# A two-layer hybrid encoder trunk in 32-bit floats: keys and gate inputs turned through memory, one offset product in the last norm, readers pinned and GpSimd in program order

## The chip, the cores and the metric

The kernel runs on one core of one Trainium2 chip. The metric is the device time of one execution in microseconds (us), as the median over several runs. TensorE (PE in the profile), VectorE (DVE), ScalarE (ACT) and GpSimd (POOL) are the core's compute engines; SyncE (SP) issues transfers, and ScalarE and GpSimd can do so as well.

## The reference, cut to what matters

Two layers of one block. One input projection feeds three groups of heads, each group is gated, and an output projection with a residual and a layer norm closes the layer.

```
for l in range(2):                                       # x: (256, 2048)
    h = x @ w_in[l]                                      # 11 slices of its columns
    y_a = softmax(q k^T / sqrt(128) + rel_bias) v        # 8 heads, chunked band
    log_g = log_sigmoid(b_lr @ gate_w + gate_b) / 16     # b_lr: 16 columns
    y_b = gated_linear_attention(b_q, b_k, b_v, log_g)   # 4 heads, chunks of 64, then RMS norm
    y_m = softmax(m_q mk^T / sqrt(128)) mv               # 4 heads, 256 memory rows
    y = concat(y_a * silu(a_z), y_b * silu(b_z), y_m * silu(m_z))
    x = layer_norm(sqrt(2) * x + y @ w_out, ln_g, ln_b)
```

In the linear attention b is the running sum of log_g in a chunk of 64 rows. The state after a chunk takes the keys times exp(b_last - b), as products over the rows, so these scaled keys must lie with the rows on the partitions. The gate product needs b_lr with its 16 columns on the partitions.

## The kernel before, in words

**Products.** Each 32-bit operand is split in a rounded high part and a low remainder: `parts(hi, lo, src)` (L122) casts on ScalarE (L124) and subtracts on VectorE (L125). A full product is three products, hi x hi, lo x hi, hi x lo (`as_products`, L266). Weights come in pieces of two 128-row blocks (`piece`, L136) with four buffers each for the raw piece, the high part and the low part. One group of 512 columns (`as_group`, L274) is 8 pieces of 12 products.

**The written order.** TensorE and SyncE issue in the order in which the program is written (`manual_schedule`, L49). The other engines are ordered by the framework's planner, which goes by priorities (weight pieces have 4000) and by its own estimate of times. `tc.keep_in_program_order(ins)` pins an instruction behind everything written before it on its engine; what is written after it may still pass it.

**The interleaving.** Every weight piece ends with `tick` (L52), which advances a clock by one, or by 388/512 in the groups of 388 columns. Small work is written as generators that are stepped by the clock: `yield n` says that the next step is due n ticks later. At most two of the queued generators run at a time, three when the linear attention is done; generators in `side` always run. `finish(gens)` ticks without any piece between until the generators are done. A layer's groups are, in order: (memory values and keys), BQK, two groups of 388 columns with values, AQ0, AK0, values, AQ1, AK1, values, MQ, then the gates BZ, AZ0, AZ1, MZ, then the output projection's groups 0 and 1 together, 2 and 3. The linear attention `gla` starts with AQ0, the heads `a_head` and `m_head` follow, `gated` multiplies each gate in, and the output projection asks for each gated part before pieces 2, 4 and 6.

**Turning data.** `turned` (L530) turns a matrix without TensorE: VectorE transposes 32x32 blocks (L535), GpSimd writes them to a DRAM tile `home` (L537), and four reads bring them back so that a column block lands on its partitions (L540). Readers then take blocks of 32. `staged` (L804) does this for a projection group and puts the reader, `placed` (L521), five ticks later. Two things in `gla` were still turned on TensorE: the gate input `lr` (L346, two transposes a layer, copied to `lrT` at L348) and the scaled keys `kd` (L399, four a layer, copied to `kdT` at L401).

**The last norm.** `norm_last` (L707) ends the kernel. For three column blocks of the second row half, TensorE adds to the centred residual the offsets, written as -mean times the gain row plus std times the bias row. The factors `nt` (128x4) are transposed (L774), split with `parts` (L778), and each block gets two products of 4 rows (L741, L742) before it is scaled by 1/std and stored.

Of the kernel before, what the change touches and what calls it, by code (L numbers as in the profile page):

```python
# [18 lines left out]
P = 128  # L19
D = 2048  # L20
T = 256
# [15 lines left out]
def hybrid_trunk_kernel(  # L37
# [66 lines left out]
    def bank():  # L104
        return psa.tile([P, 512], F32, name=nm("bk"), tag="bk")
# [15 lines left out]

    def parts(hi, lo, src):  # L122

        act.copy(hi, src)  # L124
        dve.tensor_tensor(lo, src, hi.bitcast(F32), op=ALU.subtract)  # L125

# [186 lines left out]

    def gla(gw, gb, ng, gq, gk, lr, asv, yraw):
        gqf = gq.rearrange("p b t -> p (b t)")
# [27 lines left out]

        pt = bank()
        for t in range(2):
            pe.transpose(pt[:, t * P:(t + 1) * P], lr[:, t].bitcast(F32), ident)  # L346
        lrT = sm.tile([P, T], F32R, name=nm("lrT"), tag="lrT")
        dve.tensor_copy(lrT, pt[:, :T])  # L348
# [23 lines left out]
        act.activation(kd, kd, AF.Exp, scale=1.0 / 16)  # L372
        dve.tensor_tensor(kd, gkf, kd, op=ALU.mult)
        eb = scratch([P, 512])
        act.activation(eb, b_, AF.Exp, scale=1.0 / 16)
# [3 lines left out]
        dve.tensor_tensor(qe, gqf, eb, op=ALU.mult)  # L379
        yield 6  # L380

# [13 lines left out]

        pt = bank()
        for t in range(2):
            for b in range(2):
                pe.transpose(pt[:, (t * 2 + b) * P:(t * 2 + b + 1) * P], kd[:, b * T + t * P:b * T + t * P + P], ident)  # L399
        kdT = scratch([P, 4, P])  # L400
        act.copy(kdT, pt.rearrange("p (g c) -> p g c", c=P))  # L401
        yield 2
        nxt = [decayed(LEVELS[0])]
        kv = [bank() for _ in range(2)]
        for c in range(3):
            rs = slice((c % 2) * 64, (c % 2) * 64 + 64)
            t = c // 2
            for b in range(2):
                for par in range(2):
                    h = 2 * b + par  # L410
                    mm(kv[c % 2][par * 64:par * 64 + 64, (t * 2 + b) * P:(t * 2 + b + 1) * P],
                       kdT[rs, t * 2 + b, par * 64:par * 64 + 64],
                       asv[rs, t, 16 + h * P:16 + (h + 1) * P], True, True)
# [79 lines left out]
    def gla_turned(yraw, ng, y):  # L493

        yT = []
        for par in range(2):
            yT.append(hd.tile([P, 4, P], F32, name=nm("yT"), tag=("gq", "gk")[par]))
            turned(P, (yT[par], yraw[:, 2 * par:2 * par + 2].rearrange("p t d -> p (t d)")))
            yield 2 + 4 * par
        for par in range(2):  # L500
            for t in range(2):
                for b in range(2):
                    hi, lo = (x.rearrange("p k (t a j) -> p k t a j", t=2, j=32)[:, b * 2 + par, t] for x in y[:2])
                    src = yT[par].rearrange("p a (t b j) -> p t b a j", t=2, j=32)[:, t, b]
                    act.activation(hi, src, AF.Copy, scale=ng[:, 0:1])
                    dve.scalar_tensor_tensor(lo, src, ng[:, 0:1], hi.bitcast(F32), op0=ALU.mult, op1=ALU.subtract)
            yield 1

    def gated(zT, yraw, heads, y):

        while not all(h in done for h in heads):
            yield 1
        for j in range(0, 4, 2):
            gz = scratch([P, 2, T])
            for t in range(2):
                z, o, r = (zT[:, t].rearrange("p a (k j) -> p k a j", j=32)[:, j:j + 2],
                           *(x[:, :, t * P:(t + 1) * P].rearrange("p k (a j) -> p k a j", j=32) for x in (gz, yraw[:, j:j + 2])))
                dve.tensor_tensor(o, z, r, op=ALU.mult)  # L518
            parts(y[0][:, j:j + 2], y[1][:, j:j + 2], gz)

# [9 lines left out]
    def turned(n, *todo):  # L530

        homes = []
        for _, src in todo:
# [3 lines left out]
            pool.dma_start(homes[-1], blocks)  # L537
        for (dst, _), home in zip(todo, homes):
            for b in range(4):
                pool.dma_start(dst[b * 32:(b + 1) * 32], home[:, b].rearrange("(a i) n -> i a n", a=4))  # L540

    SCALE = P ** -0.5

    def a_head(h, load_bias, bias, q, k, asv, y):

        if h + 2 < 8:
            load_bias(h + 2)
        pb = bank()
# [16 lines left out]
        turned(96, (pT, s))  # L565
        yield 9
        po = bank()
        v0 = 528 + h * P
# [6 lines left out]
    def m_head(h, q, mk, mv, y, laid):  # L575
# [22 lines left out]
        turned(128, (pT, s.rearrange("p t m -> p (t m)")))  # L598
        yield 7
        ph, pl = scratch([P, 2, 256], F32R), scratch([P, 2, 256], F32R)  # L600
        for t in range(2):
            parts(*(x.rearrange("p m (t a j) -> p t m a j", t=2, j=32)[:, t] for x in (ph, pl)),
                  pT.rearrange("p a (t m j) -> p t m a j", t=2, j=32)[:, t])
        yield 2
# [86 lines left out]

    def norm_rows(l):

        rows = []
        for i in range(2):
# [4 lines left out]
            pool.dma_start(raw[1:2], ln_b[l:l + 1, cs])  # L700
            parts(hi[:2], lo[:2], raw[:2])
            pool.dma_start(both[0:2], hi[:2])
            pool.dma_start(both[2:4], lo[:2])
            rows.append(both)
        return rows

    def norm_last(accs, rest, stats, gb, rows, more):  # L707
# [16 lines left out]
        def scales(t, meanwhile):  # L724
# [4 lines left out]
            if t == 1:  # L729
                dve.tensor_scalar(nt[:, 0:4:2], mvt[t][:, 0:1].to_broadcast([P, 2]), -1.0, None, op0=ALU.mult)  # L730
            meanwhile()
# [3 lines left out]
            if t == 1:  # L735
                dve.scalar_tensor_tensor(nt[:, 1:4:2], v.to_broadcast([P, 2]), -2.0, rstd[t].to_broadcast([P, 2]),
                                         op0=ALU.mult, op1=ALU.mult)

        def offsets(i, hl, o):
            cs = slice(i % 2 * 512, i % 2 * 512 + 512)  # L740
# [13 lines left out]
        with tc.manual_schedule(engines={DVE, mybir.EngineType.Activation}):  # L754
# [7 lines left out]
            with tc.high_priority(AHEAD):  # L762
# [10 lines left out]
                pt = bank()  # L773
                pe.transpose(pt[:4, :P], nt, ident)  # L774
                result(n, 1, 0, 256)
                centred(n, 1, 256, 512)
                hl = nparts[:4, 0], nparts[:4, 1]
                parts(*hl, pt[:4, :P])  # L778
                result(n, 1, 256, 512)
                for i in (1, 0, 2):  # L780
                    offsets(i, hl, o[i])
                    r = res[:, 1, columns(i)]
# [17 lines left out]
    for l in range(L):  # L800
# [3 lines left out]
        def staged(g, x, raw, place):  # L804
# [16 lines left out]
        else:  # L821
# [4 lines left out]
            raw = hd.tile([P, 4, T], F32, name=nm("qk"), tag="qk", bufs=4)  # L826
            mkey = staged(G_MK, memq, raw, lambda src, at: parts(at(mk[0]), at(mk[1]), src))
            finish(gens[:1])
# [5 lines left out]
        def place(src, at):  # L834
            act.mul(at(gq), src[:, :2], 0.125)
            dve.tensor_copy(at(gk), src[:, 2:])

# [19 lines left out]
        for i in (0, 32):  # L857
            act.copy(lr[:, :, i:i + 16], asv[:, :, :16])
        dve.tensor_tensor(lr[:, :, 16:32], asv[:, :, :16], lr[:, :, :16].bitcast(F32), op=ALU.subtract)
        values(1)  # L860
        if l == 0:
# [12 lines left out]
        finish(early_gens)  # L874
        gens = [[gla(*gp, gq, gk, lr, asv, yraw[0])]]
        waiting.extend(gens[0])
        linear[:] = gens[0]
        for half in range(2):
            q, k = (hd.tile([P, 4, T], F32, name=nm("qk"), tag="qk", bufs=4) for _ in range(2))
            laid = staged(G_AQ0 if half == 0 else G_AQ1, xq, yraw[3], lambda src, at, q=q: act.copy(at(q), src))  # L880
            laid += staged(G_AK0 if half == 0 else G_AK1, xq, k, None)
            values(2 + half)
            finish(laid)
# [3 lines left out]
        q = [hd.tile([P, 4, T], F32R, name=nm("mq"), tag="qk", bufs=4) for _ in range(2)]  # L887
        laid = staged(G_MQ, xq, yraw[3], lambda src, at: parts(at(q[0]), at(q[1]), src))
        gens.append([m_head(h, q, mk, mv, yraw[3][:, h], laid) for h in range(4)])
# [10 lines left out]
        for i, g in ((1, G_AZ0), (2, G_AZ1), (3, G_MZ)):  # L900
# [19 lines left out]

        rows = norm_rows(l) if last else None
        for n in range(WO_N):
# [141 lines left out]
```

## Time and profile before

| | before |
|---|---|
| median of 3 runs | 907.57 us (907.14 to 911.58) |
| profiled execution, own time | 906.32 us |
| its span, first to last instruction | 904.5 us |
| mean granted TensorE clock | 0.998 |
| TensorE busy | 897.8 us (99%) |
| VectorE / ScalarE / GpSimd busy | 607.2 / 477.2 / 197.8 us |

Busy time is the share in which an engine executes; a line such as L102 is a line of the kernel, and since nearly all products go through one helper they share one line, so they are told apart by the tiles they write and read. In the list of waits, the first name is the engine and tile that waited, the name behind the arrow is what it waited for, and the numbers are the total in us, how often, and the longest.

### The profile page before, as it was taken

What the parts mean: (1) busy time and instruction counts of PE and PEld (TensorE: products, weight loads), DVE (VectorE), ACT (ScalarE), POOL (GpSimd) and SP (SyncE); (2) the same over time, 40 slices, a digit from 0 to 9 for tenths busy, and PEclk for the clock granted to TensorE, in tenths of its full rate; (3) what the DMA queues carried; (4) which work ended last, traced back from release to release, by engine and by line L of the source; (5) the groups of instructions that cost most, each with busy time, mean ns of one, the idle gap of its engine ahead of it and who ended that gap; (6) DMA issues with size and microseconds to landing.
All of it is one profiled execution on the core that took longest, in us unless ns stands there. A gap on an engine that the chain in (4) does not pass through costs nothing.

```text
span 904.5 us, 13856 instructions
## 1 busy us (share of the span) xinstructions
PE 897.8 (99%) x4798; PEld 768.2 (85%) x4798; DVE 607.2 (67%) x878; ACT 477.2 (53%) x687; POOL 197.8 (22%) x369
## 2 busy tenths in 40 slices
PE   9999999999999999999999999999999999999997
PEld 8889988988988888888888898898898888888885
DVE  6765478766566676565587676777756586666766
ACT  6654465574545566433476445655744465655440
POOL 0002012116243553200000220221071434334000
PEclk9999999999999999999999999999999999999999
DMA  9977976858977998776675687658698879888652
GB/s 308 324 210 212 310 234 183 262 167 259 273 230 224 265 275 264 232 254 192 210 247 192 201 250 224 203 186 249 189 267 242 261 218 276 253 260 274 211 164 93
DMA packets 145974, 211.34 MB, mean 234 GB/s; under 512 B 15464, under 2 KB 117224, under 8 KB 145648
## 3 DMA queue, kind: packets, MB, share of 16 engines
q1 hardware_dynamic: 130544, 173.28, 61.5%
q0 software_dynamic: 15072, 36.79, 14.3%
q8 instruction: 37, 0.61, 0.3%
q10 hardware_dynamic: 288, 0.39, 0.1%
q14 instruction: 33, 0.27, 0.1%
HBM read 192.02 MB, written 18.35 MB: 233 GB/s over the span
## 4 chain that ended last, share of the span: by engine, by line
PE 99%; DMA 0%; DVE 0%; ACT 0%; issue 0%
PE acc L102 90%; PE bk L102 8%; PE bk L630 0%; DMA raw<-w 0%; PE bk L399 0%; ACT res L786 0%; DVE stats L771 0%; PE bk L346 0%; DVE res L770 0%; ACT wh L124 0%; DVE res L722 0%; DVE mvt L725 0%; PE bk L774 0%; ACT nparts L124 0%; DVE rs_u L733 0%
## 5 line engine op out<-in xcount | busy, mean ns | idle before, releaser
L102 PE MATMUL acc<-wh,x 128*128 128x512 f32 (+2 forms) x2452 | 736.9, 382 | 0.2 <-ACT wh L124 0.2
L102 PEld LDWEIGHTS acc<-wh,x 128*128 128x128 f32 x2452 | 453.7, 188 | 73.5 <-ACT wh L124 0.5
L125 DVE TENSOR_TENSOR wl<-raw,wh 128x1024 fp32r<-128x1024 f32 (+3 forms) x321 | 368.1, 1152 | 196.9 <-ACT wh L124 194.3
L124 ACT CAST wh<-raw 128x1024 fp32r<-128x1024 f32 (+3 forms) x321 | 318.7, 996 | 327.9 <-PE acc L102 250.4
L102 PE MATMUL acc<-wl,x 128*128 128x512 f32 (+2 forms) x1226 | 465.0, 380 | 0.0
L102 PEld LDWEIGHTS acc<-wl,x 128*128 128x128 f32 x1226 | 230.4, 188 | 39.1 <-DVE wl L125 0.4
L537 POOL DMA_DIRECT2D home<-sc x66 | 36.9, 560 | 455.0 <-DVE sc L535 447.0
L540 POOL DMA_DIRECT2D pT<-home x96 | 52.7, 555 | 46.4 <-DMA home<-sc 19.3
L540 POOL DMA_DIRECT2D qk<-home x56 | 30.5, 551 | 13.3 <-DMA home<-sc 7.9
L540 POOL DMA_DIRECT2D zT<-home x48 | 26.2, 553 | 29.9 <-DMA home<-sc 19.3
L540 POOL DMA_DIRECT2D yr<-home x48 | 26.1, 551 | 20.2 <-DMA home<-sc 14.8
L535 DVE STREAM_TRANSPOSE sc<-sc 128x512 f32<-128x512 f32 (+1 forms) x36 | 22.7, 643 | 2.0 <-ACT sc L906 1.4
L560 ACT ACTIVATE sc<-sc,mx 128x128 f32<-128x128 f32 (+1 forms) x32 | 14.4, 450 | 16.3 <-DVE mx L558 16.2
L535 DVE STREAM_TRANSPOSE sc<-acc 128x512 f32<-128x512 f32 x26 | 17.0, 692 | 6.9 <-PE acc L102 6.9
L518 DVE TENSOR_TENSOR sc<-zT,yr 128x256 f32<-128x256 f32 x24 | 8.9, 417 | 13.8 <-DMA zT<-home 13.8
L124 ACT CAST x<-sc 128x512 fp32r<-128x512 f32 x20 | 11.8, 616 | 4.4 <-DVE sc L518 3.1
L125 DVE TENSOR_TENSOR x<-sc,x 128x512 fp32r<-128x512 f32 x20 | 13.2, 686 | 0.7 <-ACT x L124 0.7
L125 DVE TENSOR_TENSOR x<-raw,x 128x1024 fp32r<-128x1024 f32 x5 | 6.1, 1212 | 11.3 <-ACT x L124 11.3
L102 PEld LDWEIGHTS bk<-pT,asv 128*128 128x128 f32 x64 | 12.0, 189 | 1.8
L391 DVE TENSOR_TENSOR sc<-gk,sc 128x512 f32<-128x512 f32 x12 | 8.3, 691 | 7.2 <-ACT sc L389 7.2
L102 PE MATMUL bk<-qk,qk 128*128 128x128 f32 (+1 forms) x64 | 13.1, 326 | 0.0
L102 PE MATMUL bk<-pT,asv 128*128 128x256 f32 (+1 forms) x64 | 13.0, 326 | 0.0
(209 smaller groups left out, 557.0 us busy)
## 6 DMA issues: line engine op xcount, KB each, us to landing
raw<-w SPq DMA_DIRECT2D x387, 256.0 KB, 4.4
raw<-w SPq DMA_DIRECT2D x62, 512.0 KB, 5.1
raw<-w SPq DMA_DIRECT2D x64, 388.0 KB, 3.9
home<-sc POOLq DMA_DIRECT2D x50, 256.0 KB, 4.8
qk<-home POOLq DMA_DIRECT2D x56, 64.0 KB, 5.7
bias<-relw SPq DMA_DIRECT2D x16, 192.0 KB, 5.2
yr<-home POOLq DMA_DIRECT2D x48, 64.0 KB, 4.2
home<-sc POOLq DMA_DIRECT2D x16, 192.0 KB, 3.2
```

The lines of the kernel that those rows point to most:

```text
L102: pe.matmul(o, l, r, start=start, stop=stop, skip_group_check=True)
L124: act.copy(hi, src)
L125: dve.tensor_tensor(lo, src, hi.bitcast(F32), op=ALU.subtract)
L391: dve.tensor_tensor(kl, gkf, dd, op=ALU.mult)
L518: dve.tensor_tensor(o, z, r, op=ALU.mult)
L535: dve.transpose(blocks.rearrange("p b (g j) -> p g b j", j=32), src.rearrange("p (g b j) -> p g b j", b=4, j=32))
L537: pool.dma_start(homes[-1], blocks)
L540: pool.dma_start(dst[b * 32:(b + 1) * 32], home[:, b].rearrange("(a i) n -> i a n", a=4))
L560: act.activation(s[:, own[t]], s[:, own[t]], AF.Exp, bias=mx[:, t:t + 1], accum_out=zs[:, t:t + 1])
```

## The change

1. The gate input is turned with a block transpose on VectorE, one write home and two reads of 32 partitions, started behind the first group of 388 columns. The gate product reads it with 64 rows in place of 128. The first step of `gla` goes.
2. The scaled keys are turned with `turned` as well; the copy into `kdT` waits 14 ticks in place of 6.
3. `turned` writes its reads two ticks after its writes; GpSimd joins the engines that issue in program order.
4. Readers of turned data are pinned (`placed_here`), and come more ticks later: 9 or 6 in place of 5 in `staged`, 10 in place of 6 for the gates, 10 in place of 7 in `m_head`, 8 more in place of 4 in `gla_turned`.
5. The bias loads move: 2 and 3 behind the groups AQ0 and AK0, 4 to 7 behind a head's scores. The row pieces of the last norm are prepared by a generator.
6. In the last norm the high and low parts of the factors are made before the transpose, so that one transpose gives 8 rows, one cast follows, and each block gets one product of 8 rows.

```diff
-    ctx.enter_context(tc.manual_schedule(engines={PE, mybir.EngineType.SP}))
+    ctx.enter_context(tc.manual_schedule(engines={PE, mybir.EngineType.SP, mybir.EngineType.Pool}))
...
+    def placed_here(ins):
+        return tc.keep_in_program_order(ins)
-    def parts(hi, lo, src):
-        act.copy(hi, src)
-        dve.tensor_tensor(lo, src, hi.bitcast(F32), op=ALU.subtract)
+    def parts(hi, lo, src, keep=lambda ins: ins):
+        keep(act.copy(hi, src))
+        keep(dve.tensor_tensor(lo, src, hi.bitcast(F32), op=ALU.subtract))
...
-        pt = bank()
-        for t in range(2):
-            pe.transpose(pt[:, t * P:(t + 1) * P], lr[:, t].bitcast(F32), ident)
-        lrT = sm.tile([P, T], F32R, name=nm("lrT"), tag="lrT")
-        dve.tensor_copy(lrT, pt[:, :T])
-        yield 2
...
-            mm(pl[:, b * T:(b + 1) * T], gw[:, b * P:(b + 1) * P], lrT, True, True)
+            mm(pl[:, b * T:(b + 1) * T].rearrange("p (t a j) -> p t a j", t=2, j=32), gw[:64, b * P:(b + 1) * P],
+               lrT.rearrange("p a (t j) -> p t a j", t=2), True, True)
...
+        kdr = hd.tile([P, 4, P], F32, name=nm("kdr"), tag="st")
+        turned(P, (kdr, kd))
...
-        yield 6
+        yield 14
...
-        pt = bank()
-        for t in range(2):
-            for b in range(2):
-                pe.transpose(pt[:, (t * 2 + b) * P:(t * 2 + b + 1) * P], kd[:, b * T + t * P:b * T + t * P + P], ident)
         kdT = scratch([P, 4, P])
-        act.copy(kdT, pt.rearrange("p (g c) -> p g c", c=P))
+        placed_here(act.copy(kdT.rearrange("p g (a j) -> p g a j", j=32), kdr.rearrange("p a (g j) -> p g a j", j=32)))
...
-            yield 2 + 4 * par
+            yield 2 + 8 * par
...
-        for (dst, _), home in zip(todo, homes):
-            for b in range(4):
-                pool.dma_start(dst[b * 32:(b + 1) * 32], home[:, b].rearrange("(a i) n -> i a n", a=4))
+        def reads():
+            for (dst, _), home in zip(todo, homes):
+                for b in range(4):
+                    pool.dma_start(dst[b * 32:(b + 1) * 32], home[:, b].rearrange("(a i) n -> i a n", a=4))
+            return
+            yield
+        side.append((reads(), now[0] + 2))
...
-        if h + 2 < 8:
-            load_bias(h + 2)
...
         yield 9
+        if h < 4:
+            load_bias(h + 4)
...
-        nparts = hd.tile([P, 2, P], F32R, name="nparts", tag="qe")
-        nt = small([P, 4], "nt1")
+        nparts = hd.tile([P, P], F32R, name="nparts", tag="qe")
+        nt = sm.tile([P, 2, 4], F32R, name="nt1", tag="nt1")
...
-                dve.tensor_scalar(nt[:, 0:4:2], mvt[t][:, 0:1].to_broadcast([P, 2]), -1.0, None, op0=ALU.mult)
+                mean = mvt[t][:, 0:1].to_broadcast([P, 2])
+                dve.tensor_scalar(nt[:, 0, 0:4:2], mean, -1.0, None, op0=ALU.mult)
+                dve.scalar_tensor_tensor(nt[:, 1, 0:4:2], mean, -1.0, nt[:, 0, 0:4:2].bitcast(F32), op0=ALU.mult, op1=ALU.subtract)
...
-                dve.scalar_tensor_tensor(nt[:, 1:4:2], v.to_broadcast([P, 2]), -2.0, rstd[t].to_broadcast([P, 2]),
-                                         op0=ALU.mult, op1=ALU.mult)
+                dve.scalar_tensor_tensor(std, v, -2.0, rstd[t], op0=ALU.mult, op1=ALU.mult)
+                dve.tensor_copy(nt[:, 0, 1:4:2], std.to_broadcast([P, 2]))
+                dve.tensor_tensor(nt[:, 1, 1:4:2], std.to_broadcast([P, 2]), nt[:, 0, 1:4:2].bitcast(F32), op=ALU.subtract)
-            mm(o, hl[0], rows[i // 2][:4, cs], False, False)
-            mm(o, hl[1], rows[i // 2][:4, cs], False, True)
+            mm(o, nparts[:8], rows[i // 2][:8, i % 2 * 512:i % 2 * 512 + 512], False, True)
...
-                pe.transpose(pt[:4, :P], nt, ident)
+                pe.transpose(pt[:8, :P], nt.rearrange("p a b -> p (a b)").bitcast(F32), ident)
+                act.copy(nparts[:8], pt[:8, :P])
...
-                hl = nparts[:4, 0], nparts[:4, 1]
-                parts(*hl, pt[:4, :P])
...
-            side.append((gen, now[0] + 5))
+            side.append((gen, now[0] + (6 if place is None else 9)))
...
+        lrT = sm.tile([64, 4, 64], F32R, name=nm("lrT"), tag="lrT")
+        blocks = scratch([P, 2, 64])
+        dve.transpose(blocks.rearrange("p b (t j) -> p t b j", j=32), lr[:, :, :64].bitcast(F32).rearrange("p t (b j) -> p t b j", j=32))
+        home = drm.tile([P, 2, 64], F32, name=nm("home"), tag="home64")
+        pool.dma_start(home, blocks)
+        def gate_reads(lrT=lrT, home=home):
+            for b in range(2):
+                pool.dma_start(lrT[b * 32:(b + 1) * 32].bitcast(F32), home[:, b].rearrange("(a i) n -> i a n", a=4))
...
+        side.append((gate_reads(), now[0] + 2))
...
-            side.extend((x, now[0] + 6) for x in need[i * 2])
+            side.extend((x, now[0] + 10) for x in need[i * 2])
...
-        rows = norm_rows(l) if last else None
+        rows = []
+        if last:
+            side.append((norm_rows(l, rows), now[0] + 10))
```

More of the change, by code (lines that the diff above doesn't have):

```diff
@@ L312, in gla_inputs, with gla @@
         return gw, gb, ng
-    def gla(gw, gb, ng, gq, gk, lr, asv, yraw):
+    def gla(gw, gb, ng, gq, gk, lrT, asv, yraw):
         gqf = gq.rearrange("p b t -> p (b t)")
@@ L411, in gla @@
                     mm(kv[c % 2][par * 64:par * 64 + 64, (t * 2 + b) * P:(t * 2 + b + 1) * P],
-                       kdT[rs, t * 2 + b, par * 64:par * 64 + 64],
+                       kdT[rs, b * 2 + t, par * 64:par * 64 + 64],
                        asv[rs, t, 16 + h * P:16 + (h + 1) * P], True, True)
@@ L504, in gla_turned @@
                     src = yT[par].rearrange("p a (t b j) -> p t b a j", t=2, j=32)[:, t, b]
-                    act.activation(hi, src, AF.Copy, scale=ng[:, 0:1])
-                    dve.scalar_tensor_tensor(lo, src, ng[:, 0:1], hi.bitcast(F32), op0=ALU.mult, op1=ALU.subtract)
+                    placed_here(act.activation(hi, src, AF.Copy, scale=ng[:, 0:1]))
+                    placed_here(dve.scalar_tensor_tensor(lo, src, ng[:, 0:1], hi.bitcast(F32), op0=ALU.mult, op1=ALU.subtract))
             yield 1
@@ L690, in norm_columns, with norm_rows @@
         return raw, hd.tile([P, 32], F32, name=nm("gbT"), tag="pairs1")
-    def norm_rows(l):
-        rows = []
+    def norm_rows(l, rows):
         for i in range(2):
@@ L700, in norm_rows @@
             pool.dma_start(raw[1:2], ln_b[l:l + 1, cs])
-            parts(hi[:2], lo[:2], raw[:2])
-            pool.dma_start(both[0:2], hi[:2])
-            pool.dma_start(both[2:4], lo[:2])
+            yield 4
+            parts(hi[:2], lo[:2], raw[:2], placed_here)
+            yield 1
+            for at in (0, 4):
+                pool.dma_start(both[at:at + 2], hi[:2])
+                pool.dma_start(both[at + 2:at + 4], lo[:2])
             rows.append(both)
-        return rows
     def norm_last(accs, rest, stats, gb, rows, more):
@@ L713, in norm_last @@
         mvt, rstd = [], []
-        nparts = hd.tile([P, 2, P], F32R, name="nparts", tag="qe")
-        nt = small([P, 4], "nt1")
+        nparts = hd.tile([P, P], F32R, name="nparts", tag="qe")
+        nt = sm.tile([P, 2, 4], F32R, name="nt1", tag="nt1")
+        std = small([P, 1], "std")
         for t in range(2):
@@ L826, in hybrid_trunk_kernel @@
             raw = hd.tile([P, 4, T], F32, name=nm("qk"), tag="qk", bufs=4)
-            mkey = staged(G_MK, memq, raw, lambda src, at: parts(at(mk[0]), at(mk[1]), src))
+            mkey = staged(G_MK, memq, raw, lambda src, at: parts(at(mk[0]), at(mk[1]), src, placed_here))
             finish(gens[:1])
@@ L834, in place @@
         def place(src, at):
-            act.mul(at(gq), src[:, :2], 0.125)
-            dve.tensor_copy(at(gk), src[:, 2:])
+            placed_here(act.mul(at(gq), src[:, :2], 0.125))
+            placed_here(dve.tensor_copy(at(gk), src[:, 2:]))
         early_gens = staged(G_BQK, xq, raw, place)
@@ L874, in hybrid_trunk_kernel @@
         finish(early_gens)
-        gens = [[gla(*gp, gq, gk, lr, asv, yraw[0])]]
+        gens = [[gla(*gp, gq, gk, lrT, asv, yraw[0])]]
         waiting.extend(gens[0])
@@ L879, in hybrid_trunk_kernel @@
             q, k = (hd.tile([P, 4, T], F32, name=nm("qk"), tag="qk", bufs=4) for _ in range(2))
-            laid = staged(G_AQ0 if half == 0 else G_AQ1, xq, yraw[3], lambda src, at, q=q: act.copy(at(q), src))
+            laid = staged(G_AQ0 if half == 0 else G_AQ1, xq, yraw[3], lambda src, at, q=q: placed_here(act.copy(at(q), src)))
+            if half == 0:
+                load_bias(2)
             laid += staged(G_AK0 if half == 0 else G_AK1, xq, k, None)
+            if half == 0:
+                load_bias(3)
             values(2 + half)
```

17 lines of the change are left out of this document (9 added, 8 removed).

## The prediction

> **What bounds the kernel now.** I read the profile's page first (shares of busy time, the forty slices, the chain that ended last), then the list of waits, then the order of time on each engine around the places that the change touches.
>
> ```profile
> span 904.5 us, 13856 instructions
> PE 897.8 (99%) x4798; PEld 768.2 (85%) x4798; DVE 607.2 (67%) x878; ACT 477.2 (53%) x687; POOL 197.8 (22%) x369
> PE 99%; DMA 0%; DVE 0%; ACT 0%; issue 0%
> 131.64 5.47 PE acc L102 x24
> ACT wh L124 <- PE acc L102: 250.4, 176, 4.3
> PE acc L102 <- ACT wh L124: 0.2, 1, 0.2
> DVE sc L518 <- DMA zT<-home: 13.8, 3, 6.2
> ACT qk L880 <- DMA yr<-home: 8.2, 4, 4.8
> ```
>
> TensorE is busy for 897.8 of 904.5 us and is 99% of the chain. A busy PE can still hide slow steps, so I looked at the pace: the chain's piece of 24 full-width products takes 5.47 us, 0.228 us each, and long runs keep that pace. The waits say the same from the other side: in the body of the kernel TensorE waits 0.2 us for a weight cast, while ScalarE waits 250.4 us in 176 places for TensorE to give a weight buffer back. The weights are ahead.
>
> How far ahead follows from the buffers. There are four of each weight buffer, and a piece is 12 products, so 12 x 0.228 = 2.73 us of TensorE. A cast begins when the piece four before it is done, which leaves three pieces, 8.2 us, for the cast and the subtraction.
>
> ```profile
> 61.19 1.05 ACT L124 CAST wh<-raw 128x1024 fp32r<-128x1024 f32 x1 [1.67 <-PE acc L102]
> 62.15 0.40 ACT L308 CAST gw<-gwraw 48x256 fp32r<-48x256 f32 x1
> 63.87 0.85 ACT L124 CAST wh<-raw 128x776 fp32r<-128x776 f32 x1 [1.32 <-PE acc L102]
> L125 DVE TENSOR_TENSOR wl<-raw,wh 128x1024 fp32r<-128x1024 f32 (+3 forms) x321 | 368.1, 1152 | 196.9 <-ACT wh L124 194.3
> ```
>
> A cast takes 1.05 us and the subtraction 1.15 us, so the second half of a piece is ready about 8.2 - 2.2 = 6 us before TensorE wants it. This 6 us is the cover on which everything below rests. The waits in front of readers that are now pinned (13.8 us before L518, 8.2 us before L880, the longest 6.2 and 4.8 us) lie inside it or at its edge, and TensorE shows no loss from them. Taking them away therefore gives nothing that can be seen; only work taken off TensorE, and the tail, can shorten the time.
>
> **Part 1: transposes off TensorE.** Each layer loses two transposes of the gate input (L346) and four of the keys (L399).
>
> ```profile
> 107.80 0.39 PE L102 MATMUL acc<-wl,x 128*128 128x512 f32 x1
> 108.03 0.62 PE L102 MATMUL acc<-wh,x 128*128 128x512 f32 x2
> 108.48 0.39 PE L102 MATMUL acc<-wl,x 128*128 128x512 f32 x1
> 108.71 0.38 PE L346 MATMUL bk<-ident,lr 128*128 128x128 f32 x2
> 108.85 0.71 PE L102 MATMUL acc<-wh,x 128*128 128x512 f32 x2
> 109.40 0.40 PE L102 MATMUL acc<-wl,x 128*128 128x512 f32 x1
> 131.04 0.60 PE L399 MATMUL bk<-ident,sc 128*128 128x128 f32 x4
> 131.39 0.70 PE L102 MATMUL acc<-wh,x 128*128 128x512 f32 x2
> 131.93 0.39 PE L102 MATMUL acc<-wl,x 128*128 128x512 f32 x1
> L399 PE MATMUL bk<-ident,sc 128*128 128x128 f32 x8 | 1.2, 272 | 0.0
> ```
>
> What counts is the distance between starts, not the 272 ns that one transpose takes from start to end. The two at L346 occupy 108.71 to 108.85, 0.14 us, and the pair of products behind them takes 0.55 us (108.85 to 109.40) where the pair ahead took 0.45 (108.03 to 108.48): 0.10 more. Together 0.24 us. The four at L399 take 131.39 - 131.04 = 0.35 us, and the pair behind them 0.54 instead of 0.45: 0.44 us. A layer saves 0.68 us and two layers 1.36; without the slow pair it would be 0.98, and if each took its full 272 ns alone, 12 x 0.272 = 3.3. I take 1.36, since the starts are what the next product sees, and keep 0.98 and 3.3 for the range. The Trainium skill, "TensorE: Matmul & The Clock Gate", section "Part 4: PE-mode transpose", puts a 128x128 transpose at about 275 ns inside a kernel; the trace agrees on the duration (272 ns), but its starts lie 0.11 us apart, and by the page's figure the sum would be the 3.3 us above. The gate products keep their number and width; half their rows are no longer loaded, which I count as nothing.
>
> **What replaces them** runs elsewhere. Per layer VectorE gains one 128x512 block transpose and a small one, and loses the copy at L348; GpSimd gains two writes home and six reads.
>
> ```profile
> L535 DVE STREAM_TRANSPOSE sc<-sc 128x512 f32<-128x512 f32 (+1 forms) x36 | 22.7, 643 | 2.0 <-ACT sc L906 1.4
> L348 DVE CAST lrT<-bk 128x256 fp32r<-128x256 f32 x2 | 0.8, 422 | 0.8 <-PE bk L346 0.8
> home<-sc POOLq DMA_DIRECT2D x50, 256.0 KB, 4.8
> qk<-home POOLq DMA_DIRECT2D x56, 64.0 KB, 5.7
> 90.92 0.19 DVE L859 TENSOR_TENSOR lr<-asv,lr 128x32 fp32r<-128x32 f32 x1
> L540 POOL DMA_DIRECT2D qk<-home x56 | 30.5, 551 | 13.3 <-DMA home<-sc 7.9
> 126.43 0.68 DVE L373 TENSOR_TENSOR sc<-gk,sc 128x512 f32<-128x512 f32 x1
> ```
>
> Gate input: it is complete at 91.11 (L859). Block transpose at most 0.64, issue 0.55, landing 4.8, two reads issued 1.1, landing 5.7: 103.9. Its product now stands where L346 stood, at 108.7: 4.8 us of room. Keys: the gate product moves from 114.4 to 108.7, so the scaled keys, ready at 127.1 before (126.43 + 0.68), are ready near 121.4; plus 0.64 + 0.55 + 4.8 + 4 x 0.55 + 5.7 = 135.3. The copy into kdT is 14 ticks behind the product, 14 x 2.73 = 38 us, so TensorE is at 146.9 and ScalarE, 8.2 us ahead of it, at 138.7: 3.4 us of room, and the products come two ticks later still. Both hidden; uncovered, each microsecond of lateness costs one on TensorE in each layer.
>
> **Part 2: order and ticks.** GpSimd in program order waits in its queue for each home write; reads now stand two ticks behind their write, so other writes pass between, and a place two ticks later in the order costs no time when nothing is queued there. The longer waits of the generators must not leave the loops that finish them running empty, for such a tick has no products to cover it. I counted: the linear generator takes 14+2+6+6+3+2 = 33 ticks instead of 27 and has 60 until its gate; the third gated group (10 ticks) has 12 pieces before its first reader, the second 8+4 = 12, the first 18. None runs empty that was not empty before. Attention heads start up to five ticks later, because three generators run at a time only when the linear one is done, and are still finished ahead of their gates. The norm's row pieces need 20 ticks behind the last gate group and have 24. The bias loads leave the heads, where the weight queue behind them stood still:
>
> ```profile
> SPq L867 <- DVE sc L553: 17.6, 3, 8.5
> ```
>
> 17.6 us of standing queue go; the four weight buffers had hidden it. All of this I cost at nothing.
>
> **Part 3: the last norm.** Three products of 4 rows go (two per block become one of 8 rows), and so does the subtraction at L125. Three small VectorE instructions come before the transpose.
>
> ```profile
> 895.90 0.16 DVE L730 TENSOR_SCALAR nt<-mvt 128x2 f32<-128x2 f32 x1
> 896.81 0.16 DVE L734 SCALAR_TENSOR_TENSOR rstd<-rs_u,rstd 128x1 f32<-128x1 f32 x1
> 897.00 0.16 DVE L736 SCALAR_TENSOR_TENSOR nt<-rs_v,rstd 128x2 f32<-128x2 f32 x1
> 897.62 0.26 ACT L124 CAST nparts<-bk 4x128 fp32r<-4x128 f32 x1 [1.49 <-PE bk L774]
> 897.92 0.81 PE L102 MATMUL bk<-gbrow,nparts 4*128 4x512 f32 x2 [0.34 <-ACT nparts L124]
> L102 PE MATMUL bk<-gbrow,nparts 4*128 4x512 f32 x4 | 1.4, 434 | 0.3 <-ACT nparts L124 0.3
> 898.77 0.69 ACT L786 ACTIVATE res<-bk,rstd 128x512 f32<-128x512 f32 x1 [0.90 <-PE bk L102]
> 899.68 0.69 ACT L786 ACTIVATE res<-bk,rstd 128x512 f32<-128x512 f32 x1 [0.22 <-PE bk L102]
> ```
>
> Dependent small instructions start 0.19 us apart (896.81 to 897.00). One extra ahead of the reciprocal and two extra behind the last scale are 3 x 0.19 = 0.57 us, so the cast moves from 897.62 to 898.19 and the first product from 897.92 to 898.49. There the pair took 0.81; one product takes 0.43 (mean 434 ns), so ScalarE's first result starts at 898.97 instead of 898.77. Its second waited 0.22 us for the pairs; now the products are done in time and it follows at 898.97 + 0.69 = 899.66, against 899.68. The tail gives 0.0 us: between -0.6, if the extra instructions fit into gaps and the first result starts at 898.4, and +0.6, if none of the products' saving arrives.
>
> **Sum.** -1.36 + 0.0 on the profiled execution, whose span of 904.5 becomes 903.1 and whose own time of 906.32 becomes about 904.9. The median of the three runs, 907.57, lies 1.25 us above that execution; the same step gives 907.57 - 1.4 = 906.2 us.
>
> **The rivals.** *Slower: the gate weights' copy gets caught behind GpSimd.* The memset of gw (L307) ran at the very start, and its reader L308 at 62.15, right behind a weight cast.
>
> ```profile
> 0.74 0.31 POOL L307 MEMSET gw<- 128x256 f32 x1 [0.29 <-POOLq L1054]
> 73.28 1.27 POOL L537 DMA_DIRECT2D home<-sc  x2 [71.98 <-DVE sc L535]
> ```
>
> In program order the memset comes behind the home writes, so not before 73.28 + 1.27 = 74.55, done at 74.9. If L308 keeps its place on ScalarE, the cast of 63.87 starts at 75.3 and ends at 76.1; TensorE wants it three pieces after 63.87, at 72.1, and stands 4 us, in each layer: 906.2 + 8 = 914 us. It decides as soon as L308 stands ahead of the casts that follow it. Against it: those casts have a high priority and the planner sees the memset's wait, so it should put them first. *Slower: a turn that lands late.* If the landings of the gate input take twice their 4.8 and 5.7 us, it is there at 114.4 instead of 108.7: 5.7 us twice, 917 us. The room of 4.8 us and an empty GpSimd queue speak against it. The Trainium skill, "VectorE: DVE Perf Modes", section "Rules for kernel authors", speaks against this step too: for a 128x128 transpose it says TensorE where PSUM will do; the trace before cannot show the new path exposed, only its room. *Faster:* TensorE idles 904.5 - 897.8 = 6.7 us in all. Were half of that to go with the steps, 906.2 - 3.4 = 902.8. Against it: no wait of TensorE in the body is long enough, and the start and the last norm keep theirs.
>
> **How the numbers follow.** The forecast gets 0.86, the caught copy 0.07, the late turn 0.04, the faster case 0.03. Half a per cent, 4.5 us, is about what a measurement of this kernel can tell from no change; only the rivals pass it. So faster 0.03, same 0.86, slower 0.11. The range runs from 906.2 - 1.9 (transposes at 3.3) - 0.6 (tail) = 903.7 up to 910.2, the caught copy in one layer alone.
>
> **What would show it.** Right: no transposes at L346 and L399, TensorE's busy time down by 1 to 2 us and its waits in the body still under a microsecond, waits of L518's and L880's successors for DMA shorter, the first cast of nparts some 0.6 us later measured from the last statistics, and the end unmoved. Wrong: a wait of TensorE for a cast near the end of the BQK group or for lrT, or a span that moves while TensorE's busy time does not.

## The result, and the profile after

| | before | after |
|---|---|---|
| median | 909.37 us (907.14 to 911.58, 6 runs) | 915.99 us (915.48 to 917.91, 6 runs) |
| profiled execution, own time | 906.32 us | 916.28 us |
| its span | 904.5 us | 914.5 us |
| mean granted TensorE clock | 0.998 | 0.993 |

The change makes the kernel slower: the ratio is 1.008, interval 1.0053 to 1.0107. The forecast was 906.2 us with a range up to 910.2.

The page after: busy time of the engines, shares of the chain that ended last.

```profile
PE 899.7 (98%) x4783; PEld 768.2 (84%) x4783; DVE 608.1 (66%) x882; ACT 480.7 (53%) x691; POOL 208.1 (23%) x389
PE 91%; DMA 5%; POOL 1%; DVE 1%; issue 1%; ACT 0%; SPq 0%; DVEq 0%; ACTq 0%
```

The waits (engine and tile, what it waited for, us in total, times, longest):

```profile
PE bk L102 <- DMA qk<-home: 6.3, 4, 2.5
PE acc L102 <- ACT wh L128: 0.3, 2, 0.2
ACT wh L128 <- PE acc L102: 263.7, 178, 3.0
```

The weights are as far ahead as before (263.7 us of ScalarE waiting for TensorE, 0.3 us the other way). New is one line: TensorE waits 6.3 us, in four places, for the reads that bring turned projections (qk) back from memory. DMA, which had 0% of the chain, now has 5%.

Where those waits lie is seen in TensorE's order of time (start, duration, instruction, count, and in brackets the idle time before and what ended it):

```profile
245.83 0.39 PE L102 MATMUL acc<-wl,x 128*128 128x512 f32 x1
247.00 0.46 PE L102 MATMUL bk<-qk,qk 128*128 128x128 f32 x2 [0.77 <-DMA qk<-home]
249.95 0.87 PE L102 MATMUL bk<-qk,qk 128*128 128x256 f32 x2 [2.49 <-DMA qk<-home]
250.27 1.41 PE L102 MATMUL acc<-wh,x 128*128 128x512 f32 x2
251.47 0.63 PE L102 MATMUL acc<-wl,x 128*128 128x512 f32 x1
...
254.11 0.63 PE L102 MATMUL acc<-wh,x 128*128 128x512 f32 x2
...
700.31 0.68 PE L102 MATMUL bk<-qk,qk 128*128 128x256 f32 x2 [2.35 <-DMA qk<-home]
```

The same scores before, and the tenth weight product behind them:

```profile
243.57 0.82 PE L102 MATMUL bk<-qk,qk 128*128 128x128 f32 x4
...
246.29 0.61 PE L102 MATMUL acc<-wh,x 128*128 128x512 f32 x2
```

It is the same place in both layers: the scores of head 4, the first reader of the second key group (AK1). TensorE stands 0.77 + 2.49 us, and then does not get back to its pace: two products from 250.27 to 251.47 are 0.60 us each, then one from 251.47 to 251.90 takes 0.43, where 0.228 is usual. From the product at 245.83 to that at 254.11 are 8.28 us; they hold 10 full products and four small ones. Before, the same stretch went from 243.34 to 246.29, 2.95 us. So layer 0 loses 5.33 us here, and layer 1 loses 5.11 (696.41 to 704.47, 8.06 us, against 2.95).

The landmarks agree. The first transpose of layer 1, before and after:

```profile
472.81 0.27 PE L618 MATMUL bk<-ident,gbrow 128*128 128x128 f32 x1
```

```profile
477.93 0.27 PE L621 MATMUL bk<-ident,gbrow 128*128 128x128 f32 x1
```

The first layer loses 477.93 - 472.81 = 5.12 us. The first product of the last norm's residual starts at 904.05 in place of 894.31, so the second layer loses 9.74 - 5.12 = 4.62, and the tail 10.0 - 9.74 = 0.26. Each layer's loss is that of the one place, less what the change saves.

Why the keys came late is read from GpSimd's queue. Before, around the write of AK1's blocks (home<-sc) and its reads (qk<-home):

```profile
223.11 1.14 POOL L537 DMA_DIRECT2D home<-sc  x2 [2.78 <-DVE sc L535]
...
226.78 2.17 POOL L540 DMA_DIRECT2D qk<-home  x4 [0.30 <-issue]
229.32 2.17 POOL L540 DMA_DIRECT2D qk<-home  x4 [0.38 <-DMA pT<-home]
```

After, first the block transposes of AK1 on VectorE, then GpSimd's queue, then the transfers as the chain that ended last lists them:

```profile
225.04 1.27 DVE L532 STREAM_TRANSPOSE sc<-acc 128x512 f32<-128x512 f32 x2
```

```profile
225.41 0.56 POOL L534 DMA_DIRECT2D home<-sc  x1 [0.49 <-DVE sc L532]
226.50 2.17 POOL L539 DMA_DIRECT2D pT<-home  x4 [0.53 <-DMA home<-sc]
230.74 2.17 POOL L539 DMA_DIRECT2D pT<-home  x4 [2.07 <-PE acc L102]
232.90 1.11 POOL L534 DMA_DIRECT2D home<-sc  x2
239.88 4.35 POOL L539 DMA_DIRECT2D qk<-home  x8 [5.87 <-DMA home<-sc]
```

```profile
232.90 6.70 DMA home<-sc
243.68 6.13 DMA qk<-home
```

The blocks are ready at 226.31 (before: 223.41), but the write is issued only at 232.90: the reads of two attention heads (pT<-home) stand ahead of it, and the second of these waited until its own write, issued at 225.41, had landed, 4.8 us later, at about 230.2 (the bracket names TensorE, one of several signals of this wait; the read cannot go before that landing in any case). The write then took 6.70 us to land, and the last read, issued at 243.68, landed at 249.81. TensorE had come to these scores at 246.06 (245.83 + 0.23).

Those heads are later than before. The scores of heads 1 and 3 (four products of 128x128 each; head 2 lies between, at 198.07 and 212.10) before and after:

```profile
194.65 0.81 PE L102 MATMUL bk<-qk,qk 128*128 128x128 f32 x4
...
210.32 0.82 PE L102 MATMUL bk<-qk,qk 128*128 128x128 f32 x4
```

```profile
208.68 0.81 PE L102 MATMUL bk<-qk,qk 128*128 128x128 f32 x4
...
215.50 0.81 PE L102 MATMUL bk<-qk,qk 128*128 128x128 f32 x4
```

A third generator may run only when the linear attention is done, and that now takes 33 ticks for 27. The trace shows it: the last products of linear attention (bk<-st,qe) start at 204.80 in place of 188.05, 16.75 us later, which is six ticks of 2.73 us and a little. So three heads spread over 16 us come in 7 us, right ahead of AK1.

### The profile page after: what moved, and what is told of

Read it like the earlier page. It is cut to its first block, busy times and chain, and to the rows that moved or that the text cites. A ratio compares the mean times of both kernels' runs of the same rounds, so it can differ in the third digit from the quotient of the medians.

```text
span 914.5 us, 13863 instructions
## 1 busy us (share of the span) xinstructions
PE 899.7 (98%) x4783; PEld 768.2 (84%) x4783; DVE 608.1 (66%) x882; ACT 480.7 (53%) x691; POOL 208.1 (23%) x389
## 4 chain that ended last, share of the span: by engine, by line
PE 91%; DMA 5%; POOL 1%; DVE 1%; issue 1%; ACT 0%; SPq 0%; DVEq 0%; ACTq 0%
PE acc L102 84%; PE bk L102 6%; DMA raw<-w 3%; DMA home<-sc 1%; DMA qk<-home 1%; POOL qk L539 1%; PE bk L633 0%; POOL pT L539 0%; ACT wh L128 0%; DVE wl L129 0%; SPq L176 0%; DVE x L129 0%; SPq L151 0%; DVE mv L129 0%; ACT res L791 0%
## 5 line engine op out<-in xcount | busy, mean ns | idle before, releaser
L129 DVE TENSOR_TENSOR wl<-raw,wh 128x1024 fp32r<-128x1024 f32 (+3 forms) x321 | 368.3, 1151 | 216.6 <-ACT wh L128 215.4
L128 ACT CAST wh<-raw 128x1024 fp32r<-128x1024 f32 (+3 forms) x321 | 318.2, 994 | 340.4 <-PE acc L102 263.7
L554 DVE SCALAR_TENSOR_TENSOR sc<-bk,bias 128x384 f32<-128x384 f32 x16 | 8.7, 543 | 14.5 <-PE bk L102 14.5
L102 PEld LDWEIGHTS bk<-qk,qk 128*128 128x128 f32 x64 | 9.6, 189 | 8.5 <-issue 6.3
L389 ACT ACTIVATE sc<-sc 128x512 f32<-128x512 f32 x12 | 7.6, 631 | 15.6 <-DVE sc L387 12.9
L129 DVE TENSOR_TENSOR x<-sc,x 128x512 fp32r<-128x512 f32 x20 | 13.7, 685 | 0.7 <-ACT x L128 0.7
L666 DVE SCALAR_TENSOR_TENSOR res<-res,acc 128x512 f32<-128x512 f32 x15 | 9.6, 681 | 5.3 <-PE acc L102 5.3
```

Of the source, the lines that this page charges most:

```text
L102: pe.matmul(o, l, r, start=start, stop=stop, skip_group_check=True)
L128: keep(act.copy(hi, src))
L129: keep(dve.tensor_tensor(lo, src, hi.bitcast(F32), op=ALU.subtract))
L389: act.activation(dd, dd, AF.Abs)
L554: dve.scalar_tensor_tensor(s, pb[:, :384], SCALE, bias[h], op0=ALU.mult, op1=ALU.add)
L666: dve.scalar_tensor_tensor(r, r, ALPHA, acc, op0=ALU.mult, op1=ALU.add)
```

## The experiments

Two causes lie in the change: **late heads** (the longer linear generator bunches them in front of AK1), and **the order** (GpSimd may no longer issue what is ready first). A third may be **late landings** (the write takes 6.7 us, perhaps because other transfers are under way). Each experiment is compared with the kernel before on the same chip. Edits are against the kernel after, unless said otherwise.

### GpSimd given back to the planner

```diff
-    ctx.enter_context(tc.manual_schedule(engines={PE, mybir.EngineType.SP, mybir.EngineType.Pool}))
+    ctx.enter_context(tc.manual_schedule(engines={PE, mybir.EngineType.SP}))
```

> The changed kernel with one edit: GpSimd is taken out of the engines that issue in program order, so the planner orders its queue as before. Theory A (in the program order, the write of the second key block K1 stands behind the reads of heads 1 to 3, one of which waits for its own landing; TensorE then waits for K1 and runs slowly for some us after the wait): the two waits of TensorE for qk<-home go, and with them about 10.6 us: span near 904, median 905 to 908. Rival B (K1 is late because the reads stand two ticks behind the write and because the bias loads now fall on the same stretch, whatever the order of the queue): at least half of the loss stays, 911 or more.

Measured: 911.41 us against 907.56, ratio 1.0042 (1.0028 to 1.0056). AK1's write and the first products that wait for its reads:

```profile
228.43 1.11 POOL L534 DMA_DIRECT2D home<-sc  x2
```

```profile
247.67 0.67 PE L102 MATMUL bk<-qk,qk 128*128 128x256 f32 x2 [1.58 <-DMA qk<-home]
...
695.31 1.19 PE L102 MATMUL bk<-qk,qk 128*128 128x256 f32 x2 [2.18 <-DMA qk<-home]
```

The write goes out 4.5 us earlier, at 228.43, but two waits for the same reads are left. The order is about half of the loss, and not the whole of it.

### The heads' reads three ticks later

```diff
-    def turned(n, *todo):
+    def turned(n, *todo, late=2):
-        side.append((reads(), now[0] + 2))
+        side.append((reads(), now[0] + late))
-        turned(96, (pT, s))
+        turned(96, (pT, s), late=5)
```

> The changed kernel, GpSimd still in program order, with one edit: the reads of an attention head's turned scores stand five ticks behind their write in place of two, so that K1's two writes come ahead of the reads of heads 2 and 3. Nothing else moves. Theory A: K1's write is issued near 229 instead of 232.9, its last read lands near 245 instead of 249.8, and TensorE's wait for it falls from 3.2 us to under 1 us in each layer: median 905 to 909. Rival B: the write's place matters little, 913 or more.

Measured: 925.28 us, ratio 1.0203 (1.0184 to 1.0223). TensorE's waits, and GpSimd's queue:

```profile
PE bk L102 <- DMA pT<-home: 14.8, 4, 6.5
```

```profile
240.40 1.63 POOL L539 DMA_DIRECT2D pT<-home  x3 [0.79 <-DMA qk<-home]
```

The wait for AK1 is gone, so the reads ahead of its write had indeed held it. But now the last of these heads' reads are behind AK1's, at 239 to 242, and TensorE waits for them, up to 6.5 us. The queue holds 20 reads and 5 writes of 0.55 us each in this stretch, and one order or the other is late: that they all come at once is the likelier fault, which the runs with early heads below test.

### The gate product over 128 rows again

```diff
-        lrT = sm.tile([64, 4, 64], F32R, name=nm("lrT"), tag="lrT")
+        lrT = sm.tile([P, 4, 64], F32R, name=nm("lrT"), tag="lrT")
+        pool.memset(lrT[64:].bitcast(F32), 0.0)
```

with all rows of gw in the product.

> The changed kernel with the gate product over 128 rows again: lrT has 128 partitions, the upper 64 set to zero by GpSimd. The waits for K1 stay. In the trace of the changed kernel the stretch from the last product before the pair to the second behind it takes 1.08 us against 0.70 before. If the half-height product is what costs this (its weight load does not start while a full-height product runs), the stretch falls back to about 0.70 us, 0.8 us over both layers. If the strided reading of lrT costs it, it stays at 1.08.

One run: 916.16 us. The gate product of after, the weight loads of its pair, and then the gate product of this kernel:

```profile
108.62 0.39 PE L102 MATMUL acc<-wl,x 128*128 128x512 f32 x1
108.94 0.50 PE L102 MATMUL bk<-lrT,gw 64*128 64x256 f32 x2
...
109.94 0.39 PE L102 MATMUL acc<-wl,x 128*128 128x512 f32 x1
```

```profile
108.94 0.29 PEld L102 LDWEIGHTS bk<-lrT,gw 64*128 64x128 f32 x2 [0.35 <-issue]
```

```profile
108.63 0.39 PE L102 MATMUL acc<-wl,x 128*128 128x512 f32 x1
108.86 0.40 PE L102 MATMUL bk<-lrT,gw 128*128 128x256 f32 x2
...
109.56 0.39 PE L102 MATMUL acc<-wl,x 128*128 128x512 f32 x1
```

From the product ahead of the pair to the third behind it are 1.32 us over 64 rows (108.62 to 109.94) and 0.93 over 128 (108.63 to 109.56). Half the rows cost 0.39 us a layer. It does not show in this kernel's time, since its waits for AK1's reads took it up (the total of these was 6.9 us for 6.3).

### The kernel before, with GpSimd in order

Against the kernel before; the last norm's row pieces are prepared by a generator as in the change, since their order needs it.

```diff
-    ctx.enter_context(tc.manual_schedule(engines={PE, mybir.EngineType.SP}))
+    ctx.enter_context(tc.manual_schedule(engines={PE, mybir.EngineType.SP, mybir.EngineType.Pool}))
-        rows = norm_rows(l) if last else None
+        rows = []
+        if last:
+            side.append((norm_rows(l, rows), now[0] + 10))
```

> The kernel before with GpSimd in program order (and with the row pieces of the last norm prepared by the generator of the changed kernel, which that order needs); transposes on TensorE, the ticks and the heads' places are those of before. Theory A1 (the order does harm only together with the longer linear generator, which moves heads 1 to 3 to right ahead of K1): K1's write comes 2 to 3 us later than before, its reads land near 240, TensorE wants them at 243.6, no wait: median 907 to 911. Rival A2 (the order alone does it): TensorE waits for K1 again, 913 to 919.

Measured: 932.19 us, ratio 1.0277 (1.026 to 1.0294). TensorE's waits:

```profile
PE bk L102 <- ACT sc L124: 5.8, 3, 2.4
PE bk L102 <- DMA pT<-home: 5.2, 1, 5.2
PE bk L102 <- DMA qk<-home: 3.5, 2, 2.0
```

Both theories fell short: 932 is above the 913 to 919 of A2, but it is A2's mechanism that came. AK1 is late again in layer 0, with the heads where they were; its write goes out at 229.76:

```profile
247.58 0.67 PE L102 MATMUL bk<-qk,qk 128*128 128x256 f32 x2 [2.04 <-DMA qk<-home]
```

The order is dear where the readers come as soon as they did before: memory heads, heads and keys all wait. This kernel also writes each read directly behind its home write. So either the longer waits of the change (its point 4) or the reads two ticks later (its point 3) pay for the order; no run tells the two apart.

### The heads early again

The linear generator gets back to 27 ticks, with the order kept, and then with the planner:

```diff
-        yield 14
+        yield 8
-        placed_here(act.copy(kdT.rearrange("p g (a j) -> p g a j", j=32), kdr.rearrange("p a (g j) -> p g a j", j=32)))
+        act.copy(kdT.rearrange("p g (a j) -> p g a j", j=32), kdr.rearrange("p a (g j) -> p g a j", j=32))
```

> The changed kernel, GpSimd in program order, with the linear generator as short as before: its wait of 14 ticks is 8, so that it takes 27 in place of 33, and the copy into kdT is not pinned. Heads 1 to 3 then start where they started before. If the shift of the heads is what the order needs to do harm, TensorE's waits for K1 go: median 905 to 908. If the order does it alone, one read of head 3 still holds K1's writes (in the kernel before with this order they were issued at 229.8 and TensorE stood 3.5 us in layer 0): 911 to 916.

> The same short linear generator and unpinned copy, and GpSimd ordered by the planner, as before. With the planner and the late heads TensorE stood 1.6 and 2.2 us for K1 (909.6 us of span). Theory (both causes out, nothing is left but the work taken off TensorE): no wait for K1, span near 904.2, median 0 to 1 us below the kernel before. Rival (the pinned readers or the reads two ticks behind cost something of their own): 2 us or more above it.

Measured: with the order 910.54 us, ratio 1.0029 (1.0015 to 1.0043); with the planner 910.23, ratio 1.0031 (1.002 to 1.0043). From the first, AK1's write and reads, and TensorE's waits:

```profile
225.47 1.11 POOL L534 DMA_DIRECT2D home<-sc  x2
229.91 4.36 POOL L539 DMA_DIRECT2D qk<-home  x8 [3.33 <-DMA home<-sc]
```

```profile
PE bk L102 <- DVE sc L393: 1.5, 1, 1.5
```

The reads go out at 229.91 instead of 239.88, and no wait for AK1 is left in either. The medians miss what the theories gave (905 to 908, and 0 to 1 us below the kernel before), because other waits came up. In the changed kernel with early heads the order costs nothing that can be told (1.0029 and 1.0031); with late heads it makes 1.0042 into 1.008. What is left in TensorE's list are two other places: linear attention, which now reaches its level products before VectorE has made their factors (L393), and the memory heads' parts (L129, 1.3 us in two places).

### The kernel before, with late heads

The test from the other side, against the kernel before, with nothing else changed:

```diff
-        yield 6
+        yield 12
```

> The kernel before with one number changed: the linear generator's wait of 6 ticks is 12, so that it takes 33 ticks as in the changed kernel. Transposes stay on TensorE, GpSimd is ordered by the planner, nothing is pinned. Theory (the longer generator by itself crowds heads 1 to 3 in front of K1's turn): TensorE waits for qk<-home, 1.5 to 4 us in each layer with the slow products behind it: 3 to 8 us above the kernel before. Rival (the late heads do harm only with the pinned readers, the late reads or the order): no wait for K1, within 1 us of the kernel before.

Measured: 921.81 us, ratio 1.0156 (1.0128 to 1.0184). Waits and the queue:

```profile
PE bk L102 <- DMA qk<-home: 3.1, 2, 1.7
PE acc L102 <- DVE wl L125: 3.1, 4, 1.1
```

```profile
227.30 2.18 POOL L540 DMA_DIRECT2D pT<-home  x4 [3.93 <-DMA home<-sc]
229.48 1.64 POOL L537 DMA_DIRECT2D home<-sc  x3
```

Six ticks in the linear generator alone bring the same wait for AK1, behind the same heads, at the same place and with the planner ordering GpSimd. So late heads are enough for the wait. They are not all of its size, as the stretch measured above shows (from the weight product ahead of AK1's first scores to the tenth behind it, from the traces' starts):

| kernel | layer 0 | layer 1 |
|---|---|---|
| before | 2.95 us | 2.95 us |
| before, late heads | 4.68 | 4.86 |
| before, GpSimd in order | 8.39 | 2.95 |
| after, GpSimd by the planner | 4.75 | 6.94 |
| after | 8.28 | 8.06 |
| after, early heads, either order | 2.95 | 2.95 |

In the changed kernel all of this loss goes with the late heads, and the order adds to it only while they are late. With the readers of before, the order can make AK1 late without them.

In the kernel before with late heads, AK1 costs 1.73 + 1.91 = 3.6 us of 914.9 - 904.5 = 10.4. The larger part lies elsewhere: TensorE also waits 3.1 us for VectorE's weight remainders, which after does not show. The profiled execution took 916.98 us and is the lowest of this kernel's runs: its rows explain no more than 916.98 - 906.32 = 10.7 us, while the medians differ by 13.8, more than the 3 to 8 of the theory.

### Towards a better version

First early heads and the planner with the gate product over 128 rows, then also a little room for the two waits that were left, and the last norm of before. The last `yield` of this diff is the one in `m_head` behind its parts:

```diff
+        nxt = [decayed(LEVELS[0])]
         kdT = scratch([P, 4, P])
...
         yield 2
-        nxt = [decayed(LEVELS[0])]
...
-        yield 2
+        yield 4
```

> The kernel with both causes out, and the gate product over 128 rows, which brought the stretch around it from 1.08 to 0.70 us in each layer: 0.8 us less than without, about 1 to 1.5 us below the kernel before (ratio near 0.999). If the waits merely move, the same as without it.

> The kernel with the short linear generator, GpSimd by the planner and the gate product over 128 rows (907.7 us of span), with its remaining waits of TensorE taken out: the memory heads' products come four ticks behind their parts in place of two, the first decay is written ahead of the copy into kdT, and the last norm is that of before (two products per block). The trace showed 2.0 us of waits at the memory heads' products and 1.6 us at the linear attention's first level. If they go and nothing follows: span near 904, 1.5 to 3 us below the kernel before less the 0.25 us of the tail already counted, ratio 0.997 to 0.999. If other waits take their place: 1.000 to 1.002.

Measured: 909.76 us, ratio 1.0021 (1.0009 to 1.0034), and then 904.49 us (904.08 to 906.08) against 908.0, ratio 0.996 (0.9946 to 0.9974). The last kernel's busy time:

```profile
PE 896.1 (99%) x4786; PEld 766.5 (85%) x4786; DVE 608.4 (67%) x880; ACT 481.5 (53%) x691; POOL 209.5 (23%) x391
```

This keeps the part of the change that takes work off TensorE (busy time 896.1 for 897.8) and has no wait of more than 0.6 us in the body (for weight casts, 0.7 us in two places). It beats both kernels. Its profiled execution gains 1.0 us (905.29 for 906.32), near the 1.36 that the transposes were worth; the median gains 3.5, and the rest lies in runs that no profile shows.

## Why the prediction was wrong, by its own steps

- **The step that failed is part 2**, order and ticks, which was put at nothing: "a place two ticks later in the order costs no time when nothing is queued there", and heads that start later but "are still finished ahead of their gates". I looked for who waits for the heads, and not for what the heads wait ahead of. The queue was not empty: 12 head reads and AK1's write met at 222 to 233. In place of nothing, the stretch behind it costs 5.33 us in layer 0 and 5.11 in layer 1, by late heads and order together; taking the six ticks back removes that wait.
- **The room that was checked was the wrong one.** I worked out 6 us for weights, 4.8 for the gate input and 3.4 for the linear keys, and all three held. AK1's room was never worked out, though its rows are in the trace before: the last read is issued at about 230.9, and TensorE comes at 243.57. With the median landing of 5.7 us that is some 7 us of room.
- **The rivals named the kind, not the place.** The late turn was the gate input's; the one that came late was the second key group's, which the change does not touch. The gate weights' copy was not caught. Late landings make it worse, but they go with the time of the write. In layer 0, issued at 222.7 to 225.5 it landed in 3.6 to 5.1 us (before, and after with early heads), issued at 228.4 to 232.9 in 5.6 to 6.8 (after with either order, before with late heads, before in order). Bias loads are not what it met in the kernel after: the last of them was issued at 228.13, and from 228.69 on SyncE issued only weight reads. No run isolated what slows the write.
- **Part 1 was mis-sized.** "The gate products keep their number and width; half their rows are no longer loaded, which I count as nothing": it costs 0.39 us a layer, so that a layer saves 0.68 - 0.39 = 0.29 us. With 128 rows the pair keeps its old price.
- **Part 3 was right in its steps.** The cast came 0.59 us later against the statistics (0.57 forecast), and the last store, behind ScalarE's second result, is issued 0.05 us earlier against them (910.09 - 904.71 = 5.38 us for 900.39 - 894.96 = 5.43). The 0.26 us that the tail lost lie behind that store, from its issue to the end (4.4 us for 4.1).

```profile
904.71 0.43 DVE L777 BATCH_NORM_STATS2 stats<-res 128x6 f32<-128x256 f32 x1
907.96 0.26 ACT L781 CAST nparts<-bk 8x128 fp32r<-8x128 f32 x1 [2.09 <-PE bk L780]
```

- **"TensorE's busy time down by 1 to 2 us"** did not show: it went from 897.8 up to 899.7, since slow products count as busy. A sum over busy time would have hidden a part of the loss; the starts showed it.

## What to carry to other kernels

When a generator is made longer, look for what was held back behind it, and where that now falls in the queue that it shares: a queue of 0.55 us an issue that is 23% busy over the kernel can still hold a write back for 6.6 us (226.31 to 232.90). Work out the room of every reader that uses the queue, not only of those that are edited. Before an engine is given its written order, the readers' waits have to be as long as its landings: here the order cost 2.8% with the old waits and with reads right behind their writes, and nothing that could be told in the changed kernel with longer waits, later reads and early heads.

## What the runs showed of the hardware

TensorE was slow after some waits, not only idle in them. The windows (busy time and count of PE, PEld, DVE, ACT and POOL, then the granted clock, the transfer engines' share and GB/s) are of the kernel after behind its 2.49 us, and of the first experiment, first around a wait of 1.58 us and then behind one of 2.18 us:

```profile
250.00:254.00 4.00, 4.00 (x11) 3.16 (x12) 2.31 (x7) 0.98 (x4) 0.00 (x0) 0.57 0.38 125
```

```profile
244.00:256.00 12.00, 10.42 (x50) 8.62 (x49) 8.35 (x18) 6.04 (x13) 1.88 (x4) 1.00 0.80 227
695.31:699.31 4.00, 4.00 (x11) 3.19 (x12) 1.95 (x7) 0.98 (x4) 0.00 (x0) 0.59 0.85 273
```

Around the wait of 1.58 us the clock stayed at 1.00. Over the 4 us behind 2.18 us it was 0.59, and behind 2.49 us 0.57; there single products took 0.43 us (251.47 to 251.90). The kernel before in order narrows it: over the 4 us behind a wait of 1.90 us (at 358.51) the clock was 1.00, behind one of 2.04 us (at 247.58) 0.61, though that one came only 0.46 us of products behind another, of 1.46 us. So in these traces a wait costs more than itself when it passes some 2 us: 3.26 us idle in layer 0 cost 5.33, while 1.47 us in the kernel before with late heads cost 1.73. The Trainium skill, "TensorE: Matmul & The Clock Gate", section "Why this matters for your kernels", asks for no idle gaps over about 3 us. The trace agrees on the kind, but here 2.0 to 2.2 us was enough.

Fewer rows made a product dearer: in the gate product's rows above, the loads of 64 rows start only after 0.35 us without a load, and the stretch takes 1.32 us in place of 0.93.
